# Values and keys of the first layer projected together at the start, and 128-column products without padding, in a two-layer hybrid attention kernel

## The chip, the cores and the metric

The kernel runs on one NeuronCore of a Trainium2 chip. The metric is the device time of one execution in microseconds, the median of several runs. Where a row is quoted, PE is the matrix engine (PEld its weight loads), ACT the scalar engine, DVE the vector engine, POOL the GpSimd engine and SP the engine whose queue issues the DMAs here.

## The reference, cut to what matters

Two layers, 512 positions, model width 1024. Each layer has one projection whose columns feed two token mixers: group A (8 heads, stick-breaking attention) and group B (8 heads, sparse attention whose keys are picked by an indexer).

```python
def hybrid_layer(x, w_in, w_out, ln_g, ln_b, rel_bias, topk):
    proj = jnp.einsum('bsd,dn->bsn', x, w_in)
    qA, kA, vA, gA, qB, kB, vB, gB, qI, kI, wI = jnp.split(proj, SPLIT_POINTS, axis=-1)
    ...
    oA = stick_breaking_attention(heads(qA, HEADS_A), heads(kA, HEADS_A), heads(vA, HEADS_A))
    oB = dsa_sparse_attention(..., qI, kI, wI, rel_bias, topk)
    mix = jnp.concatenate([oA * jax.nn.silu(gA), oB * jax.nn.silu(gB)], axis=-1)
    y = jnp.einsum('bsm,md->bsd', mix, w_out)
    return layer_norm(ALPHA * x + y, ln_g, ln_b)

# indexer, in dsa_sparse_attention: keys kI (64 columns), head weights wI (8 columns)
rel = jax.nn.relu(jnp.einsum('bqhd,bsd->bqhs', qib, k_idx))
score = jnp.einsum('bqhs,bqh->bqs', rel, wib)      # top 128 keys of each query are kept
```

## The kernel before, in words

**Numbers.** Every product is made of three fp32r products: high part by high part, low by high, high by low. A high part is a copy through ACT, a low part a subtraction on DVE or POOL. XH and XL hold x in both parts, turned, in 8 slices of 128 model columns (kc). The matrix engine loads 128 columns of weights per product and streams 128 to 512 columns past them.

**Units.** The projection is done in units of 256 columns, named by group, half and kind, such as ("A", 0, "v"), and "ki", which is the indexer's 64 key columns with its 8 head-weight columns. `project_t` (line 248) makes a unit turned, with x moving (512 columns a product, 24 products per 128 columns: 8 slices by three). `project_v` (line 259) makes values with the weights moving, 256 columns a product and 96 products a unit. In the second layer (l = 1) the unit ("A", 0, "v") is made at the end of the layer before, together with the keys, as 256 + 72 = 328 moving columns; its split weights lie in `joined`, a view on the AT tiles. In the first layer (l = 0) the keys are a unit of their own of 72 weight columns and the values come later among the fills.

**Start of the first layer** (`first_units`, line 351). Nine products on zeros run first. Then x, the key weights and the two halves of ("I", 0, "q") are loaded in pieces (1, 1, 2, 2, 2 slices) and split and multiplied slice by slice into three accumulators (two of `ppj`, one of `po`). `evac_ki` and `evac_q` copy the results out; a copy of the keys to the other 64 partitions is a DMA (`twin`). The 8 head weights are turned by four small transposes (L484) and `signs` makes their signs and magnitudes.

**Slots.** After `fill(0)`, a layer runs 24 index slots and 64 attention slots. Slot s issues two products z (L430, L433: queries against keys, n = 128 (qb + 1) columns but at least 256), and the older blocks' transposes and copies. Four blocks make a head, whose values product (L599) is eight products of 512, 384, 256 and 256 columns; the last pair needs only 128, and the rest of it is held at zero by four memsets in `constants`. Between them `fill` issues projection steps up to a target that `pins` sets: a unit (16 steps of three products) is to be done by the slot in HEAD_PINS, A_PINS (another row for each layer) and B_PINS; `PREFILL = 6` steps go ahead of slot 0.

**Values of group A** are differences of neighbouring rows: `shift_values` moves the copy V_NOW by one row into V_PREV with three DMAs, and `value_steps` (SHIFT_SLOTS = 2 slots later) subtracts on DVE and splits. The order on PE, ACT, DVE and POOL is the order of the code; the SP queue's is set by the scheduler. Weights are loaded two pieces ahead (`Stream`).

```python
accs = [ppj.tile([P, S], F32, tag="pj", name="pj") for _ in range(2)]
...
nn = max(self.n, 256)
...
pins = [(0, PREFILL * 648)]
```

Of the kernel before, what the change touches and what calls it, by code (L numbers as in the profile page):

```python
# [49 lines left out]
PREFILL = 6  # L50
# [7 lines left out]
A_PINS = ((27.8, 31.2, 35, 38.2, 42, 45.4, 48.4, 51.4, 54.2, 56.8), (29, 32.5, 36, 40, 44, 47.4, 50.6, 53.8, 56.8))  # L58
SHIFT_SLOTS = 2
# [4 lines left out]
def fills(l):  # L64

    units = [("I", 1, "q"), ("A", 0, "k"), ("A", 0, "q")]
    units += [("A", 0, "v")] * (l == 0)
# [3 lines left out]
    return list(zip(units, HEAD_PINS + A_PINS[min(l, 1)] + B_PINS, strict=True))  # L71


UNITS = [("I", 0, "q")] + [u for u, _ in fills(0)]
# [18 lines left out]
def tile_hybrid(ctx: ExitStack, tc: tile.TileContext, xt, x, w_in, w_ki, w_out, ln_g, ln_b, rel_bias, onehot, out, depth=DEPTH):  # L93
# [119 lines left out]
    def units(l):  # L213
        u = [u for u, _ in fills(l)]
        return ["ki", ("I", 0, "q")] + u if l == 0 else [("A", 0, "v"), "ki", ("I", 0, "q")] + u

    specs, index = [], {}
    for l in range(depth):
        for unit in units(l):
# [28 lines left out]
    def project_t(l, unit, evac):  # L248
        n = 72 if unit == "ki" else P
        for c in range(1 if unit == "ki" else 2):  # L250
            w = stream.get(index[l, unit] + c)
            acc = ppj.tile([P, S], F32, tag="pj", name="pj")[:n]
            for kc in range(KC):
                mm3(acc, [t[:, kc * n : (kc + 1) * n] for t in w], kc, kc == 0, kc == KC - 1)
# [4 lines left out]
    def project_v(l, unit, vt, keys=None):  # L259
# [9 lines left out]
        for tb in range(NTB):  # L269
# [4 lines left out]
            for kc in range(KC):  # L274
# [11 lines left out]
                if (tb, kc) == (NTB - 1, KC - 1) and unit[0] == "A":  # L286
                    later.append(shift_values)
                    pending.append([SHIFT_SLOTS, lambda: value_steps(vv)])
# [62 lines left out]
    def first_units(evac_ki, evac_qi):  # L351
        done = []
        raws = kp.tile([P, 4, S], F32, tag="k", name="raws").rearrange("p a b -> p (a b)")
        raws = [vp.tile([P, NTB, 4 * P], F32, tag="v", name="raw0").rearrange("p a b -> p (a b)"), raws[:, :1024], raws[:, 1024:]]
        for i in range(3):
            done.append(tuple(wp.tile([P, 1024], F32R, tag=tag, name=f"{tag}{i}") for tag in ("whi", "wlo")))
        bias["oh"] = kp.tile([P, 4, S], F32, tag="k", name="oh").rearrange("p a b -> p (a b)")
        accs = [ppj.tile([P, S], F32, tag="pj", name="pj") for _ in range(2)]
# [5 lines left out]
        accs.append(po.tile([P, S], F32, tag="o", name="pjo"))  # L364
        cuts = [0, 1, 2, 4, 6, 8]
        for a, b in zip(cuts, cuts[1:]):
            load_x(a, b - a)
            for i in range(3):
                n = specs[i][1] // 8
                nc.sync.dma_start(raws[i][:, a * n : b * n], specs[i][0][:, a * n : b * n])  # L370
        stream.loaded = stream.ready = 3
        stream.load(4)
        for a, b in zip(cuts, cuts[1:]):
            for kc in range(a, b):
                split_x(kc)
                if kc == a:
                    for i in range(3):
                        n = specs[i][1] // 8
                        c = slice(a * n, b * n)
                        split(done[i][0][:, c], done[i][1][:, c], raws[i][:, c], lo_engine=G)  # L380
                for i in range(3):
                    n = specs[i][1] // 8
                    mm3(accs[i][:n], [t[:, kc * n : (kc + 1) * n] for t in done[i]], kc, kc == 0, kc == KC - 1)
            if a == 0:
                constants()
            if b == 6:
                stream.prep(3, V)
        for i in range(3):
            stream.done[i] = done[i]
        evac_ki(0, accs[0][:72])  # L390
        for c in range(2):
            evac_qi(c, accs[c + 1])
        stream.prep(4)
# [28 lines left out]
    class Block:  # L422
# [3 lines left out]
        def product(self, q, slot, k, ks, mask=None, cols=None, spare=False):  # L426
            nn = max(self.n, 256)
# [567 lines left out]
```

## Time and profile before

| | |
|---|---|
| median of 3 runs | 664.27 us (663.07 to 664.74) |
| the profiled execution | 663.7 us, of which the span is 661.9 us |
| granted PE clock | 0.997 of full |
| PE busy | 650.0 us, 98% of the span, 3549 products |
| DVE, ACT, POOL busy | 73%, 53%, 55% |
| start: first product on data to first z of slot 0 | 4.65 to 29.07 us |
| z products, first layer, first to last | 29.1 to 292.4 us |
| z products, second layer, first to last | 364.6 to 615.4 us |

A product's duration in a row overlaps its neighbours (0.39 us for one of 512 columns); what it costs in a row of products is the distance from its start to the next start. "Idle before" is time in which the engine stood still.

### The profile page before, as it was taken

To read this page: it belongs to the slowest core of one execution; us is meant where nothing else is said; L and a number is where in the kernel's file an instruction comes from. 1 tells how busy PE (TensorE), PEld (TensorE's weight loads), DVE (VectorE), ACT (ScalarE), POOL (GpSimd) and SP (SyncE) were. 2 spreads that over 40 slices of the span, in tenths; PEclk is the share of its full clock that TensorE was granted. 3 is DMA by queue.
4 is the path that set the end of the run, shared out by engine and by line. 5 is a ranking of instruction groups with operands and counts; after the bars stand their busy time and mean duration, and the time that the engine had idled before them with its cause. 6 is when DMAs were issued, how large, how long until landed. Compare 5 with 4: busy or idle time off the path is not lost.

```text
span 661.9 us, 10351 instructions
## 1 busy us (share of the span) xinstructions
PE 650.0 (98%) x3549; PEld 552.7 (83%) x3549; DVE 483.2 (73%) x1026; ACT 351.3 (53%) x708; POOL 361.7 (55%) x345
## 2 busy tenths in 40 slices
PE   8999999999999999999999999999999999999995
PEld 4778988988889989878898888889888898897785
DVE  3588989999956455656853789999989565556577
ACT  4586445544346566884133865544534566668700
POOL 5343634466575767788124435445466566677621
PEclk9999999999999999999999999999999999999998
DMA  7625224142243454343004242332124424442202
GB/s 260 219 79 150 97 96 127 65 128 82 78 144 97 135 125 154 101 153 98 25 21 123 97 130 94 128 96 96 64 64 144 127 81 154 138 138 71 96 33 95
DMA packets 27115, 72.85 MB, mean 110 GB/s; under 512 B 5140, under 2 KB 8084, under 8 KB 27064
## 3 DMA queue, kind: packets, MB, share of 16 engines
q1 hardware_dynamic: 27064, 72.20, 34.5%
q8 instruction: 28, 0.46, 0.3%
q14 instruction: 23, 0.19, 0.1%
HBM read 58.87 MB, written 2.31 MB: 92 GB/s over the span
## 4 chain that ended last, share of the span: by engine, by line
PE 80%; ACT 6%; DVE 6%; POOL 3%; issue 2%; DMA 2%; SPq 1%; DVEq 0%; POOLq 0%; ACTq 0%
PE pj L244 14%; PE pj L246 14%; PE pj L245 14%; PE o L599 5%; PE tr L438 4%; PE pjv L276 4%; PE pjv L277 4%; PE pjv L278 4%; PE pjo L697 4%; PE pjo L695 4%; PE pjo L694 4%; PE z L430 4%; PE z L433 3%; POOL wlo L195 2%; ACT whi L193 1%
## 5 line engine op out<-in xcount | busy, mean ns | idle before, releaser
L195 POOL TENSOR_TENSOR wlo<-raw,whi 128x512 fp32r<-128x512 f32 x158 | 215.1, 1383 | 131.2 <-ACT whi L193 125.3
L244 PE MATMUL pj<-XH,whi 128*128 128x512 f32 (+1 forms) x448 | 182.3, 407 | 0.0
L245 PE MATMUL pj<-XL,whi 128*128 128x512 f32 (+1 forms) x448 | 175.5, 392 | 1.1 <-DVE XL L149 1.1
L246 PE MATMUL pj<-XH,wlo 128*128 128x512 f32 (+1 forms) x448 | 175.8, 392 | 0.0
L246 PEld LDWEIGHTS pj<-XH,wlo 128*128 128x128 f32 (+1 forms) x448 | 83.7, 187 | 19.6 <-POOL wlo L149 0.4
L245 PEld LDWEIGHTS pj<-XL,whi 128*128 128x128 f32 (+1 forms) x448 | 84.2, 188 | 14.9 <-DVE XL L149 2.7
L244 PEld LDWEIGHTS pj<-XH,whi 128*128 128x128 f32 (+1 forms) x448 | 84.0, 188 | 14.0 <-ACT whi L148 0.7
L193 ACT ACTIVATE whi<-raw 128x1024 fp32r<-128x1024 f32 x80 | 84.1, 1054 | 4.9 <-DMA raw<-in_w_in_dram 3.3
L618 DVE TENSOR_TENSOR_SCAN om<-om 128x128 f32<-128x128 f32 (+1 forms) x64 | 71.2, 1113 | 5.8 <-POOL om L614 5.6
L612 ACT ACTIVATE om<-z 128x128 f32<-128x128 f32 (+1 forms) x64 | 28.0, 437 | 87.2 <-PE z L433 82.9
L276 PE MATMUL pjv<-whi,XH 128*128 128x256 f32 x224 | 66.3, 296 | 0.0
L278 PE MATMUL pjv<-wlo,XH 128*128 128x256 f32 x224 | 63.2, 282 | 0.0
L277 PE MATMUL pjv<-whi,XL 128*128 128x256 f32 x224 | 63.2, 282 | 0.0
L510 POOL TENSOR_TENSOR M<-M,mixt 64x512 f32<-64x512 f32 x22 | 32.0, 1454 | 47.3 <-DVE mixt L509 41.3
L741 DVE MAX8 m<-scores 128x8 f32<-128x256 f32 (+2 forms) x96 | 52.8, 550 | 0.2
L742 DVE MATCH_REPLACE8 scores<-m,scores 128x256 f32<-128x256 f32 (+2 forms) x96 | 52.1, 543 | 0.0
L614 POOL TENSOR_SCALAR_AFFINE_SELECT om<-om 128x128 f32<-128x128 f32 x64 | 22.9, 359 | 52.4 <-ACT om L612 46.4
L599 PE MATMUL o<-AT,vt 128*128 128x256 f32 (+2 forms) x256 | 48.3, 328 | 0.7 <-DVE AT L449 0.5
L599 PEld LDWEIGHTS o<-AT,vt 128*128 128x128 f32 x256 | 41.8, 188 | 6.7 <-DVE AT L449 1.5
L694 PE MATMUL pjo<-whi,XH 128*128 128x512 f32 (+1 forms) x118 | 46.3, 393 | 0.0
L449 DVE TENSOR_TENSOR AT<-tr,AT 128x128 fp32r<-128x128 f32 (+1 forms) x64 | 31.3, 489 | 20.5 <-ACT AT L446 20.0
L697 PE MATMUL pjo<-wlo,XH 128*128 128x512 f32 (+1 forms) x118 | 44.8, 380 | 0.0
(153 smaller groups left out, 1313.1 us busy)
## 6 DMA issues: line engine op xcount, KB each, us to landing
raw<-in_w_in_dram SPq DMA_DIRECT2D x68, 512.0 KB, 3.3
k<-k SPq DMA_DIRECT2D x32, 256.0 KB, 5.3
raw<-in_w_out_dram SPq DMA_DIRECT2D x14, 512.0 KB, 3.3
gbias<-f_dram SPq DMA_DIRECT2D x16, 256.0 KB, 6.1
XN<-in_x_dram SPq DMA_DIRECT2D x4, 512.0 KB
M<-M SPq DMA_DIRECT2D x4, 448.0 KB
out_dram<-XN SPq DMA_DIRECT2D x7, 256.0 KB
XN<-in_xt_dram SPq DMA_DIRECT2D x3, 512.0 KB
```

The costliest lines, as they stand in the source:

```text
L193: A.activation(hi, src, AF.Copy)
L195: lo_engine.tensor_tensor(lo[:, c], src[:, c], hi[:, c], ALU.subtract)
L244: T.matmul(o, w[0], XH[:, :, kc, :], start=first, stop=False)
L245: T.matmul(o, w[0], XL[:, :, kc, :], start=False, stop=False)
L246: T.matmul(o, w[1], XH[:, :, kc, :], start=False, stop=last)
L276: T.matmul(full, XH[:, tb, kc, :], whi, start=kc == 0, stop=False)
L277: T.matmul(full, XL[:, tb, kc, :], whi, start=False, stop=False)
L278: T.matmul(full, XH[:, tb, kc, :], wlo, start=False, stop=kc == KC - 1)
L599: T.matmul(self.o[:, q0 * P :], vt[:, sb, self.hh * P : (self.hh + 1) * P], at_block(self.at[j], sb, q0, NTB - q0), start=n == 0, stop=n == 7)
L618: V.tensor_tensor_scan(rev, rev, rev, 1.0, ALU.mult, ALU.min)
L694: T.matmul(acc[:, cols], XH[:, tb, m, :], whi, start=n == 0, stop=False)
L697: T.matmul(acc[:, cols], XH[:, tb, m, :], wlo, start=False, stop=n == 2 * len(mts))
```

## The change

Three things change. First, the first layer begins with ("A", 0, "v") and the keys together, 328 columns with the weights moving, and ("I", 0, "q") beside them, all three loaded, split and multiplied slice by slice; the unit "ki" of 72 weight columns, the four small transposes and the fill of ("A", 0, "v") go, four transposes of the keys come in. The signs are made as soon as the keys are out. Second, the value steps of that unit run at slot 14, both layers have one row of A_PINS, and the first layer's PREFILL is 8. Third, products whose result is 128 columns wide stream 128 columns instead of 256, and the memsets of the padding go.

```diff
-PREFILL = 6
+PREFILL = (8, 6)
...
-A_PINS = ((27.8, 31.2, 35, 38.2, 42, 45.4, 48.4, 51.4, 54.2, 56.8), (29, 32.5, 36, 40, 44, 47.4, 50.6, 53.8, 56.8))
-SHIFT_SLOTS = 2
+A_PINS = (29, 32.5, 36, 40, 44, 47.4, 50.6, 53.8, 56.8)
+SHIFT_SLOTS = (14, 2)
...
-        for i in range(2):
-            for j in range(2):
-                V.memset(at_block(AT[i][j], 3, 2, 1).bitcast(F32), 0.0)
...
+        cuts = [0, 1, 2, 3, 4, 6, 8]
         for a, b in zip(cuts, cuts[1:]):
             load_x(a, b - a)
+            half, at = specs[unit[0] + a // 4][0], a % 4
+            nc.sync.dma_start(vk_raw[:, a:b, :W256], half[:, at * W256 : (at + b - a) * W256].rearrange("p (a b) -> p a b", b=W256))
+            nc.sync.dma_start(vk_raw[:, a:b, W256:], specs[unit[1]][0][:, a * 72 : b * 72].rearrange("p (a b) -> p a b", b=72))
+            nc.sync.dma_start(q_raw[:, :, a * P : b * P], q_src[:, :, a * P : b * P])
...
+        def product(j, kc, w, q):
+            x = (XH, XL, XH)[j]
+            first, last = kc == 0 and j == 0, kc == KC - 1 and j == 2
+            for tb in range(NTB) if q is None else ():
+                T.matmul(full[tb], x[:, tb, kc, :], w[j // 2][:, kc % 4, :], start=first, stop=last)
+            for c in q or ():
+                T.matmul(q_accs[c].rearrange("p (a b) -> p a b", b=P), q_w[c][j // 2][:, kc * P : (kc + 1) * P], x[:, :, kc, :], start=first, stop=last)
...
+            if b >= 6:
+                stream.prep(stream.ready, V if b == 6 else G)
+        for j in range(3):
+            product(j, KC - 1, w, None)
+        for tb in range(NTB):
+            V.tensor_copy(keys[:, tb, :], full[tb][:, W256:])
+            A.activation(V_NOW[:, tb, :], full[tb][:, :W256], AF.Copy)
+        shift_values()
+        head_weights()
+        for c in range(2):
+            for j in range(3):
+                product(j, KC - 1, w, (c,))
+            if c == 0:
+                turn_keys(keys)
+        for c in range(2):
+            evac_qi(c, q_accs[c])
...
-            nn = max(self.n, 256)
+            nn = self.n
...
-                for n, (sb, q0, j) in enumerate((sb, q0, j) for sb, q0 in ((0, 0), (1, 1), (2, 2), (3, 2)) for j in range(2)):
+                for n, (sb, q0, j) in enumerate((sb, q0, j) for sb, q0 in ((0, 0), (1, 1), (2, 2), (3, 3)) for j in range(2)):
...
         if l == 0:
-            first_units(evac_ki, lambda c, p: evac_q(qi, c, p))
+            first_units(nxt["keys"], turn_keys, head_weights, lambda c, p: evac_q(qi, c, p))
+            pending.append([SHIFT_SLOTS[0], lambda: value_steps(nxt["v"].rearrange("p t (a r) -> p t a r", r=256))])
```

**Order on PE, one slice of the start.** Before, the nine products of a slice (pj of 72 rows are the keys, the others the two halves of the queries):

```order
L244 MATMUL pj<-XH,whi_124 72x512
L245 MATMUL pj<-XL,whi_124 72x512
L246 MATMUL pj<-XH,wlo_125 72x512
L244 MATMUL pj<-XH,whi_126 128x512
L245 MATMUL pj<-XL,whi_126 128x512
L246 MATMUL pj<-XH,wlo_127 128x512
L244 MATMUL pjo<-XH,whi_128 128x512
L245 MATMUL pjo<-XL,whi_128 128x512
L246 MATMUL pjo<-XH,wlo_129 128x512
```

Now the 18 of a slice (AT_105 and AT_106 are the split weights of values and keys, whiq and wloq those of the queries):

```order
L378 MATMUL pjv<-AT_105,XH 128x328 x4
L380 MATMUL pjq<-XH,whiq_125 128x512
L380 MATMUL pjq<-XH,whiq_127 128x512
L378 MATMUL pjv<-AT_105,XL 128x328 x4
L380 MATMUL pjq<-XL,whiq_125 128x512
L380 MATMUL pjq<-XL,whiq_127 128x512
L378 MATMUL pjv<-AT_106,XH 128x328 x4
L380 MATMUL pjq<-XH,wloq_126 128x512
L380 MATMUL pjq<-XH,wloq_128 128x512
```

Three products of the keys became twelve that make the keys and the values.

**Order on PE, end of the start.** Before, behind the fills ahead of slot 0 (tw are the head weights, z the first products of slot 0):

```order
L244 MATMUL pj<-XH,whi_274 128x512
L245 MATMUL pj<-XL,whi_274 128x512
L246 MATMUL pj<-XH,wlo_275 128x512
L484 MATMUL tw<-ident,wt 128x8 x4
L430 MATMUL z<-ki,q 128x256
L433 MATMUL z<-ki,q 128x256
```

Now, the last slice (pk are the keys, turned):

```order
L378 MATMUL pjv<-AT_107,XH 128x328 x4
L378 MATMUL pjv<-AT_107,XL 128x328 x4
L378 MATMUL pjv<-AT_108,XH 128x328 x4
L380 MATMUL pjq<-XH,whiq_125 128x512
L380 MATMUL pjq<-XL,whiq_125 128x512
L380 MATMUL pjq<-XH,wloq_126 128x512
L496 MATMUL pk<-ident,keys 64x128 x4
L380 MATMUL pjq<-XH,whiq_127 128x512
L380 MATMUL pjq<-XL,whiq_127 128x512
L380 MATMUL pjq<-XH,wloq_128 128x512
L238 MATMUL pj<-XH,whi_336 128x512
```

The transposes stand between the last products of the two halves of the queries; 24 fill products follow them, and then the first z, where there were 18 fill products and the four small transposes.

**Order on SP, from the last loads of the start to the copy of the keys.** Before:

```order
L174 DMA raw_166<-in_w_in_dram 128x1024
L174 DMA raw_168<-in_w_in_dram 128x1024
L415 DMA XN<-in_x_dram 128x1024 x2
L174 DMA raw_279<-in_w_in_dram 128x1024
L415 DMA XN<-in_x_dram 128x1024 x2
L152 DMA ki<-ki 64x1024
```

Now (M<-M are the three moves of `shift_values`):

```order
L170 DMA raw_172<-in_w_in_dram 128x1024
L170 DMA raw_174<-in_w_in_dram 128x1024
L435 DMA XN<-in_x_dram 128x1024 x2
L170 DMA raw_341<-in_w_in_dram 128x1024
L435 DMA XN<-in_x_dram 128x1024
L170 DMA raw_376<-in_w_in_dram 128x1024
L435 DMA XN<-in_x_dram 128x1024
L292 DMA M<-M 1x16x48
L290 DMA M<-M 112x1024
L291 DMA M<-M 15x1024
L148 DMA ki<-ki 64x1024
```

The copy of the keys now stands behind the three moves of the values and one more load of weights.

## Rows read from the trace of the kernel before

**Rows 1.** The profile page: busy time of PE, and the chain of work that ended last, by engine.
```profile
PE 650.0 (98%) x3549; PEld 552.7 (83%) x3549; DVE 483.2 (73%) x1026; ACT 351.3 (53%) x708; POOL 361.7 (55%) x345
...
PE 80%; ACT 6%; DVE 6%; POOL 3%; issue 2%; DMA 2%; SPq 1%; DVEq 0%; POOLq 0%; ACTq 0%
```
**Rows 2.** Busy time by stretch (us from the span's start): the start; a stretch of the second layer's first attention slots. Columns: length, then PE, PEld, DVE, ACT and POOL busy, granted PE clock, DMA share, GB/s.
```profile
4.60:29.05 24.45, 23.09 (x96) 15.76 (x94) 13.14 (x26) 12.52 (x28) 13.13 (x18) 1.00 0.81 280
400.00:425.00 25.00, 25.00 (x120) 20.60 (x119) 24.45 (x56) 13.13 (x23) 13.91 (x17) 1.00 0.26 87
```
**Rows 3.** Timeline of PE in the start (start us, us, instruction): the first product on data, two of a row of four equal ones (three starts apart), and the small transposes with slot 0's first product.
```profile
4.65 0.92 PE L244 MATMUL pj<-XH,whi 128*72 128x512 f32 x1
...
8.69 0.39 PE L246 MATMUL pj<-XH,wlo 128*72 128x512 f32 x1
...
9.37 0.39 PE L246 MATMUL pj<-XH,wlo 128*128 128x512 f32 x1
...
28.73 0.41 PE L484 MATMUL tw<-ident,wt 8*128 8x8 f32 x4
29.07 0.38 PE L430 MATMUL z<-ki,q 128*128 128x256 f32 x1
```
**Rows 4.** Who waited for whom in the start, 4.6 to 29 us: engine and line, what it waited for, us in total, times, longest.
```profile
ACT whi L193 <- DMA raw<-in_w_in_dram: 3.3, 1, 3.3
PEld pj L245 <- DVE XL L149: 2.7, 4, 1.2
```
**Rows 5.** Timeline of PE in the second layer's values with keys: products of 328 columns, 38 apart, the four transposes of its keys, and the second of the 512-column products behind them.
```profile
343.20 0.32 PE L276 MATMUL pjv<-AT,XH 128*128 128x328 f32 x1
...
348.95 0.32 PE L278 MATMUL pjv<-AT,XH 128*128 128x328 f32 x1
...
350.48 0.60 PE L474 MATMUL pk<-ident,keys 128*64 128x128 f32 x4
...
351.15 0.39 PE L245 MATMUL pj<-XL,whi 128*128 128x512 f32 x1
```
**Rows 6.** Timeline of ACT in the start: when the pieces of x and the weights came and what a split costs.
```profile
3.73 0.63 ACT L148 ACTIVATE XH<-XN 128x512 fp32r<-128x512 f32 x1 [1.71 <-DMA XN<-in_xt_dram]
...
5.05 0.31 ACT L148 ACTIVATE whi<-raws 128x128 fp32r<-128x128 f32 x1 [0.34 <-DMA raws<-in_w_in_dram]
9.57 0.63 ACT L148 ACTIVATE XH<-XN 128x512 fp32r<-128x512 f32 x1 [2.15 <-DMA XN<-in_xt_dram]
...
17.04 1.06 ACT L193 ACTIVATE whi<-raw 128x1024 fp32r<-128x1024 f32 x1 [3.31 <-DMA raw<-in_w_in_dram]
```
**Rows 7.** The second layer's keys and values: copies out (ACT), the moves and the copy of the keys (SP, issue times), the value steps (DVE).
```profile
349.57 0.39 ACT L283 ACTIVATE M<-pjv 128x256 f32<-128x256 f32 x1 [2.29 <-DVE keys L281]
351.12 0.59 ACT L467 ACTIVATE ki<-pk 64x512 fp32r<-64x512 f32 x1 [0.22 <-PE pk L474]
...
346.35 0.58 SPq L299 DMA_DIRECT2D M<-M  x1
350.30 0.55 SPq L297 DMA_DIRECT2D M<-M  x1
350.90 0.89 SPq L298 DMA_DIRECT2D M<-M  x1
...
351.74 0.68 DVE L468 TENSOR_TENSOR ki<-pk,ki 64x512 fp32r<-64x512 f32 x1 [1.95 <-ACT ki L467]
357.90 1.22 DVE L302 TENSOR_TENSOR M<-M 128x1024 f32<-128x1024 f32 x1
359.82 1.29 DVE L308 TENSOR_TENSOR vt<-M,vt 128x512 fp32r<-128x512 f32 x2 [0.70 <-ACT vt L306]
```
**Rows 8.** DMA issues: count, KB each, median us from issue to landing.
```profile
k<-k SPq DMA_DIRECT2D x32, 256.0 KB, 5.3
ki<-ki SPq DMA_DIRECT2D x2, 256.0 KB, 3.0
```
**Rows 9.** Timeline of PE in two attention slots of group B, first an fp32r product of 256 columns, then a bf16 product (the mask) of 128 columns in the first slot and of 256 in the second, then (left out) the second fp32r product of 256 columns, and the transposes.
```profile
267.70 0.28 PE L430 MATMUL z<-k,q 128*128 128x256 f32 x1
267.82 0.23 PE L432 MATMUL z<-mask,identb 128*128 128x128 bf16 x1
...
268.06 0.49 PE L438 MATMUL tr<-ident,p 128*128 128x128 f32 x3
...
269.82 0.28 PE L430 MATMUL z<-k,q 128*128 128x256 f32 x1
269.94 0.28 PE L432 MATMUL z<-mask,identb 128*128 128x256 bf16 x1
...
270.18 0.60 PE L438 MATMUL tr<-ident,p 128*128 128x128 f32 x4
```
**Rows 10.** Timeline of PE where plain fp32 (not fp32r) goes over 128 columns: one product, which has two records.
```profile
40.05 0.38 PE L408 MATMUL pf<-oh 32*8 32x128 f32 x2
```
**Rows 11.** The z products of each layer (L430), duration and first and last start: the index slots and the attention slots of the first layer, then of the second.
```profile
L430 PE MATMUL z<-k,q x64: 276/308/403, 68.1 to 292.4; 128*128 128x256 f32 x32, 128*128 128x384 f32 x16, 128*128 128x512 f32 x16
L430 PE MATMUL z<-ki,q x24: 278/337/446, 29.1 to 56.1; 128*128 128x256 f32 x8, 128*128 128x384 f32 x8, 128*128 128x512 f32 x8
...
L430 PE MATMUL z<-k,q x64: 276/308/403, 401.8 to 615.4; 128*128 128x256 f32 x32, 128*128 128x384 f32 x16, 128*128 128x512 f32 x16
L430 PE MATMUL z<-ki,q x24: 277/335/397, 364.6 to 389.8; 128*128 128x256 f32 x8, 128*128 128x384 f32 x8, 128*128 128x512 f32 x8
```

More of the change, by code (lines that the diff above doesn't have):

```diff
@@ L70, in fills @@
     units += [("B", 0, "v"), ("B", 1, "k"), ("B", 1, "q"), ("B", 1, "v")]
-    return list(zip(units, HEAD_PINS + A_PINS[min(l, 1)] + B_PINS, strict=True))
-UNITS = [("I", 0, "q")] + [u for u, _ in fills(0)]
+    return list(zip(units, HEAD_PINS + A_PINS + B_PINS, strict=True))
+UNITS = [("A", 0, "v"), ("I", 0, "q")] + [u for u, _ in fills()]
 def unit_col(u):
@@ L211, in prep_ahead @@
             self.prep(self.want)
-    def units(l):
-        u = [u for u, _ in fills(l)]
-        return ["ki", ("I", 0, "q")] + u if l == 0 else [("A", 0, "v"), "ki", ("I", 0, "q")] + u
+    units = [("A", 0, "v"), "ki", ("I", 0, "q")] + [u for u, _ in fills()]
     specs, index = [], {}
     for l in range(depth):
-        for unit in units(l):
+        for unit in units:
             index[l, unit] = len(specs)
@@ L376, in first_units @@
                 if kc == a:
[L377 to L383, printed above, removed]
+                    split(w[0][:, a % 4 : a % 4 + b - a, :], w[1][:, a % 4 : a % 4 + b - a, :], vk_raw[:, a:b, :], lo_engine=G)
+                    for c in range(2):
+                        A.activation(q_w[c][0][:, a * P : b * P], q_raw[:, c, a * P : b * P], AF.Copy)
+                    for c in range(2):
+                        G.tensor_tensor(q_w[c][1][:, a * P : b * P], q_raw[:, c, a * P : b * P], q_w[c][0][:, a * P : b * P], ALU.subtract)
+                if kc < KC - 1:
+                    for j in range(3):
+                        product(j, kc, w, None)
+                        product(j, kc, w, range(2))
             if a == 0:
                 constants()
[L386 to L390, printed above, removed]
-        for c in range(2):
-            evac_qi(c, accs[c + 1])
-        stream.prep(4)
+            if b >= 6:
[7 more added lines that the diff above has]
+        head_weights()
+        for c in range(2):
+            for j in range(3):
+                product(j, KC - 1, w, (c,))
+            if c == 0:
+                turn_keys(keys)
+        for c in range(2):
+            evac_qi(c, q_accs[c])
     bias = {}
@@ L451, in tile_hybrid, with new_values @@
     turn = {"at": 0}
+    nxt = {}
+    def new_values():
+        nxt["v"] = vp.tile([P, NTB, 4 * P], F32R, tag="v", name="vt")
+        nxt["keys"] = tp.tile([P, S], F32, tag="t", name="keys")[:, : NTB * 72].rearrange("p (a b) -> p a b", b=72)
     def layer(l):
@@ L474, in turn_keys @@
                 T.transpose(p[:64, tb * P : (tb + 1) * P], keys[:, tb, :64], ident)
[L475 removed]
+            evac_ki(p)
         def head_weights():
[L478 to L487 removed]
+            tv = nxt["keys"][:, :, 64:]
             V.tensor_scalar(sgn, tv, 0.0, 2.0, ALU.is_ge, ALU.mult)
@@ L702, in layer @@
         queue, total = [], 0
-        pins = [(0, PREFILL * 648)]
-        for unit, by in fills(l):
+        pins = [(0, PREFILL[min(l, 1)] * 648)]
+        for unit, by in fills():
             total += 16 * 648
@@ L765, in layer @@
         fill(0)
[L766 removed]
+        if l:
+            head_weights()
         o0 = index[l, "o"]
@@ L928, in layer @@
             unit = ("A", 0, "v")
[L929 to L930 removed]
+            new_values()
             gen = project_v(l + 1, unit, nxt["v"], nxt["keys"])
```

65 lines of the change are left out of this document (24 added, 41 removed).

## The prediction

> **What bounds the kernel now.** I read the page first: PE is busy for 98% of the span and holds 80% of the chain that ended last [rows 1]. So the question is what PE has to do and where it stands still. By stretches, the start (4.6 to 29 us) is where it stands still: 23.1 us busy of 24.45, with the DMA engines 81% busy at 280 GB/s, and the clock is full there [rows 2]. The timeline gives what a product costs in a row: 512 columns, three starts in 0.68 us, 0.227 us [rows 3]; 328 columns, 38 starts in 5.75 us, 0.151 us [rows 5]; 256 columns, 0.120 us from one start to the next [rows 9]. These lie on a line of 0.107 us per 256 columns.
>
> From the first product on data (4.65) to slot 0's first z (29.07) are 24.42 us [rows 3]. In it are 8 slices of 9 products and 18 fill products, 90 by 0.227 = 20.43, and the small transposes, 0.34 [rows 3]. The rest, 3.65 us, is PE waiting: for low parts of x on DVE, which come late because ACT waits for x and for the next weights [rows 4, 6]. From slot 0 on, PE waits for almost nothing: the first layer takes 263.3 us from its first to its last z, the second 250.8 [rows 11], and the 12.5 between them are the 96 values products that the first makes there (96 by 0.120 = 11.5) and the bias table. That both layers pace alike in spite of different pins says that pins and DVE (24.45 of 25 us busy in the first attention slots [rows 2]) do not set the pace; PE's work does.
>
> **The change, part by part.** Sum against the profiled execution, 663.7 us.
>
> *Keys without products of their own.* 24 products of 512 columns go: 24 by 0.227 = 5.45 us less.
>
> *Values earlier and wider.* 96 products of 256 columns become 96 of 328: 96 by (0.151 - 0.120) = 3.0 us more. The second layer's rows price them exactly, since it makes the same product [rows 5].
>
> *Transposes.* The small ones go (0.34 [rows 3]); four of the keys come, priced by the second layer's: 351.15 - 350.48 less one product of 0.227 = 0.44 [rows 5]. Together 0.1 more.
>
> *The waits of the start.* A slice is now 12 by 0.151 and 6 by 0.227 = 3.17 us of PE where it was 2.04, while its data grow from 420 to 548 KB, 1.96 us at 280 GB/s [rows 2]. PE becomes the slowest. I check the places where it could still wait. The third slice of x is the ninth DMA as before, when the ninth had come by 9.57 [rows 6]; PE wants it at 5.1 + 2 by 3.17 = 11.4, and ACT needs 0.63 for x, some 0.46 for 328 columns (estimate between 0.31 for 128 and 0.63 for 512) and 0.62 for the queries in between [rows 6]. The next weights came at 17.04 [rows 6]; 1.05 MB more ahead of them is 3.7 us, so 20.8; their split (1.06), then x's and the pair of slices behind it bring the seventh slice to about 23.3, and PE wants it at 24.1. So the 3.65 us go; what could stay is 1.5 at most, if those weights are that much later. The memsets that go were DVE's; that is counted here.
>
> *A later first product.* ACT has x's first high part at 4.36 and the last weights piece came at 5.05 [rows 6]. Values and keys are now the second and third DMA, so they are in before that: some 4.6 plus 0.46 = 5.1, 0.45 later than now. Bounds: 0, and 0.9 if the pieces come as late as the fourth does.
>
> *The copy of the keys and the SP queue.* This is what is late next. The last values product ends at 5.1 + 7 by 3.17 + 1.8 = 29.1. ACT copies the values out (4 by 0.39), so 30.7; then SP issues the three moves, 0.58, 0.55 and 0.89 [rows 7], and only at 32.7 the copy of the keys, whose parts are ready at 32.0 (0.59 on ACT and 0.68 on DVE behind the copies [rows 7]). It lands 3.0 us later, as that copy does now, or 5.3, as the copies of other keys do in pairs [rows 8]: 35.7 to 38.0. PE reaches slot 0 at 29.1 + 6 by 0.227 + 0.44 + 24 by 0.227 = 36.35. The wait is 0 to 1.65; I take 0.7, nearer to the row of that very copy. PREFILL = 8 is already in it: with 6 steps PE would be there 1.4 us earlier. Behind z on PE is everything, so this wait counts in full.
>
> *Value steps at slot 14, signs at once.* 1.22 and 1.29 us of DVE [rows 7] move between index scores. Four relu tiles give PE a lead of about three slots, which are 27.0/23 = 1.17 us each [rows 11], 3.5 us against 2.5. Cost nothing; without that cover up to 2.5. The signs leave DVE's way before slot 0; PE did not wait for them. The splits of these weights leave POOL's and ACT's fills; both have room.
>
> *128 columns for 256.* Per layer and head, two z products and the last two values products: 128 products. No fp32r product under 256 columns is in the trace. The nearest row is the mask product: of 128 columns it and the second z take 268.06 - 267.82 = 0.24 us, of 256 columns 270.18 - 269.94 = 0.24 [rows 9]. Half the columns saved nothing there, because the fp32r product behind must load its weights, and that does not hide behind 128 columns. In the changed order 110 of the 128 stand ahead of an fp32r product, 12 ahead of transposes and 6 ahead of the mask. I give the 110 nothing and the 18 up to half a 256-column step, 0.053: 0 to 0.95, taken as 0.5 less. Bounds from farther rows: 128 by 0.053 = 6.8 less if nothing but columns counted, and 128 by 0.107 = 13.7 more if a narrow product cost what one of 512 does.
>
> The Trainium skill ("TensorE: Matmul & The Clock Gate", section "Back-to-back issue gap") gives about 81 ns per product for a stream of loads and products at 128 columns; by it this term would be, as an estimate, 128 by 0.039 = 5.0 us less and the time 654.2. The same page, section "LDWEIGHTS (loading the stationary operand)", has a load take its columns divided by 1.2 GHz, 107 ns for 128, which would leave an estimated 128 by 0.013 = 1.7 less and 657.5; the mask rows [rows 9] are on the side of this second rule.
>
> Sum: -5.45 + 3.0 + 0.1 - 3.65 + 0.45 + 0.7 - 0.5 = -5.35, so 658.35. A second way: slot 0 at 37.05, then 250.8 as in the second layer, plus 1.0 for the bias table, less two steps made ahead (1.36), puts the last z of the first layer at 287.5 instead of 292.4: 4.9 less, and 0.5 for the narrow products, 5.4. The profiled execution lies 0.6 under the median of the runs shown, within their spread; I add half of that: **658.7 us**.
>
> **The rivals.**
>
> *Narrow fp32r products are slow (slower than before).* One mechanism, in every first block and every values product: below 256 columns fp32r loses its rate. For it: on this engine a plain fp32 product of 128 columns has two records that last 0.38 us, where an fp32r one of 256 columns lasts 0.28 [rows 9, 10], so a rate per type exists; and nothing in the trace shows fp32r narrow. Against: the mask and three transposes of 128 columns (0.49 us together) show no such step [rows 9]. Price 0.107 each as for 512 columns: 658.7 + 0.5 + 13.7 = 672.9. It decides from (5.35 - 0.5)/128 = 0.038 on: the change is slower if a 128-column product takes more than 0.158 us.
>
> *The waits come back.* The copy of the keys lands at 38.0 (0.95 more than counted) and the value steps at slot 14 hold z for their 2.5 us: 658.7 + 3.45 = 662.1. For: DVE was at its limit later on, SP issues in order. Against: the lead of three slots.
>
> *Narrow products are cheap.* Only columns count: 0.120 - 0.053 = 0.067 us each, so 6.8 less in place of 0.5, 652.4. For: from 512 to 256 columns the price falls by columns alone. Against: the mask rows, directly. The Trainium skill's section "Back-to-back issue gap" leads most of the way here, to its 654.2.
>
> **How the numbers follow.** The forecast 0.71, slow narrow products 0.11, returning waits 0.13, cheap narrow products 0.05. About 0.3% (2 us) is what a measurement of this kernel can tell from no change. Returning waits reach less than 2 us of gain in about half of their cases: faster 0.71 + 0.05 + 0.07 = 0.83, same 0.06, slower 0.11. The forecast's best end (no later first product, no wait for the keys, 0.95 for the narrow products) is 6.95 less, about 657.0; its worst (0.9, 1.65, nothing for the narrow ones, 1.5 of waits left) is 1.95 less, 662.0. With the runs' own spread I give 656.2 to 662.2, which takes in the returning waits and leaves out the two cases on narrow products, 0.16.
>
> **What would show it.** The first z of slot 0 at 36 to 38 us, the last z of the first layer near 287.5; first products on data near 5.1 and no PE wait of over 0.3 us from there to 29; PE waiting for the copy of the keys under 1 us; a narrow z or values product starting 0.11 to 0.12 us before the next fp32r one. Starts 0.2 us apart would make the prediction wrong on the slow side, 0.07 on the other; a first z after 39 or PE waiting for relu near slot 14 would say that the waits came back.

## The result and the profile after

The changed kernel takes 661.18 us (median of 5 runs, 660.61 to 661.96), the kernel before, beside it on the same chip, 664.74 (663.07 to 665.5): ratio 0.9949, 95% interval 0.9938 to 0.996. That is 3.6 us faster, where 5.6 were forecast (664.27 to 658.7); 661.18 lies inside the range, 2.5 above the forecast. The two profiled executions differ by less than the medians do (spans 660.2 and 661.9 us): the one of after is the slowest of its five, the one of before lies under the median of its runs. A second run of the same kernel (below) gave 661.54.

PE's share on the page, against [rows 1]:

```profile
PE 646.4 (98%) x3521; PEld 551.8 (84%) x3525; DVE 481.7 (73%) x1025; ACT 350.9 (53%) x709; POOL 358.2 (54%) x344
...
PE 73%; DVE 11%; ACT 7%; issue 4%; POOL 3%; DMA 1%; DVEq 0%; POOLq 0%; ACTq 0%
```

PE's busy time went down by 3.6 us (four of the 3525 products have no record here), and its share of the chain from 80% to 73%: more of the chain now runs through DVE. The busy time by stretch, for the start (here to 37.10 us, when PE has finished the fills ahead of slot 0) and the same attention stretch as in [rows 2]:

```profile
4.60:37.10 32.50, 32.50 (x174) 28.88 (x172) 13.58 (x29) 16.28 (x36) 18.74 (x22) 1.00 0.82 272
400.00:425.00 25.00, 25.00 (x123) 20.64 (x122) 24.44 (x54) 13.43 (x24) 12.50 (x16) 1.00 0.32 105
```

PE is busy for all 32.5 us: the 3.65 us of waits of the start are gone, with the DMA engines 82% busy (81% before). The timeline of PE, with the counterparts of [rows 3] and [rows 5], and the places where it now waits:

```profile
4.77 1.53 PE L378 MATMUL pjv<-AT,XH 128*128 128x328 f32 x4
...
6.79 0.77 PE L378 MATMUL pjv<-AT,XL 128*128 128x328 f32 x4
...
29.23 0.76 PE L378 MATMUL pjv<-AT,XH 128*128 128x328 f32 x4
...
36.91 0.39 PE L240 MATMUL pj<-XH,wlo 128*128 128x512 f32 x1
38.76 0.36 PE L450 MATMUL z<-ki,q 128*128 128x256 f32 x1 [1.46 <-DMA ki<-ki]
...
60.36 0.44 PE L450 MATMUL z<-ki,q 128*128 128x384 f32 x1 [0.25 <-ACT relu L557]
...
84.98 0.33 PE L458 MATMUL tr<-ident,om 128*128 128x128 f32 x1 [0.52 <-DVE om L631]
```

Four products of 328 columns take 1.53 us at first and 0.77 from 6.79 us on, so PE began at the lower of its two rates. The granted clock of that stretch reads 1.00 all the same: at the start of a run the column does not show the slow rate, only the products' times do. PE was ready for the first z at 36.91 + 0.23 = 37.14 and got it at 38.76, 1.62 us later, behind the copy of the keys. Who waited for whom in that stretch, against [rows 4]:

```profile
ACT whi L189 <- DMA raw<-in_w_in_dram: 3.1, 1, 3.1
...
PE z L450 <- DMA ki<-ki: 1.5, 1, 1.5
```

The line "PEld pj <- DVE XL" of before is gone; ACT still waits 3.1 us for the next weights, but PE no longer waits behind it. SP's issues at the end of the start show why the keys are late:

```profile
30.97 0.62 SPq L292 DMA_DIRECT2D M<-M  x1
31.64 0.58 SPq L290 DMA_DIRECT2D M<-M  x1
32.26 0.93 SPq L291 DMA_DIRECT2D M<-M  x1
33.30 1.06 SPq L148 DMA_DIRECT2D ki<-ki  x1
```

The copy is issued at 33.30 (forecast 32.7), and z starts 5.46 us after that (forecast 3.0 to 5.3). The z products of each layer, against [rows 11]:

```profile
L450 PE MATMUL z<-k,q x64: 220/308/450, 77.3 to 291.0; 128*128 128x128 f32 x16, 128*128 128x256 f32 x16, 128*128 128x384 f32 x16, 128*128 128x512 f32 x16
L450 PE MATMUL z<-ki,q x24: 278/371/497, 38.8 to 65.3; 128*128 128x256 f32 x8, 128*128 128x384 f32 x8, 128*128 128x512 f32 x8
...
L450 PE MATMUL z<-k,q x64: 220/308/442, 400.4 to 613.8; 128*128 128x128 f32 x16, 128*128 128x256 f32 x16, 128*128 128x384 f32 x16, 128*128 128x512 f32 x16
L450 PE MATMUL z<-ki,q x24: 277/335/398, 363.1 to 388.4; 128*128 128x256 f32 x8, 128*128 128x384 f32 x8, 128*128 128x512 f32 x8
```

The first layer takes 252.2 us from its first to its last z of this line (263.3 before), the second 250.7 (250.8 before). The first z comes 9.7 us later and the last one of the first layer 1.4 us earlier. Against before's 263.3 less 96 by 0.120 for the values and 1.36 for two steps made ahead, 250.4, the first layer is 1.8 us long, and three waits in it hold 1.4: 0.36 us at 43.5 us, 0.52 at 60.36 and 0.74 at 84.98, less the 0.22 that the second layer has at the last place. These waits and those for relu and DVE below are taken from the ends of neighbouring products, against the same products in a row without a wait; the idle time in brackets is 0.2 to 0.3 us less.

### The profile page after: what moved, and what is told of

Same layout as the page of the kernel before. It is cut to its first block, busy times and chain, and to the rows that moved or that the text cites. A ratio compares the mean times of both kernels' runs of the same rounds, so it can differ in the third digit from the quotient of the medians.

```text
span 660.2 us, 10292 instructions
## 1 busy us (share of the span) xinstructions
PE 646.4 (98%) x3521; PEld 551.8 (84%) x3525; DVE 481.7 (73%) x1025; ACT 350.9 (53%) x709; POOL 358.2 (54%) x344
## 4 chain that ended last, share of the span: by engine, by line
PE 73%; DVE 11%; ACT 7%; issue 4%; POOL 3%; DMA 1%; DVEq 0%; POOLq 0%; ACTq 0%
PE pj L238 11%; PE pj L240 11%; PE pj L239 11%; PE o L612 4%; PE tr L458 4%; PE pjo L707 4%; PE pjo L710 4%; PE pjo L708 4%; PE pjv L269 3%; PE pjv L271 3%; PE pjv L270 3%; PE z L453 3%; PE z L450 3%; PE pjv L378 2%; DVE scores L755 2%
## 5 line engine op out<-in xcount | busy, mean ns | idle before, releaser
L238 PE MATMUL pj<-XH,whi 128*128 128x512 f32 x432 | 177.2, 410 | 0.0
L240 PE MATMUL pj<-XH,wlo 128*128 128x512 f32 x432 | 169.6, 393 | 0.0
L239 PE MATMUL pj<-XL,whi 128*128 128x512 f32 x432 | 168.9, 391 | 0.0
L240 PEld LDWEIGHTS pj<-XH,wlo 128*128 128x128 f32 x432 | 81.1, 188 | 18.5
L238 PEld LDWEIGHTS pj<-XH,whi 128*128 128x128 f32 x432 | 81.4, 188 | 12.3
L239 PEld LDWEIGHTS pj<-XL,whi 128*128 128x128 f32 x432 | 81.7, 189 | 11.4
L269 PE MATMUL pjv<-whi,XH 128*128 128x256 f32 x192 | 57.8, 301 | 0.0
L271 PE MATMUL pjv<-wlo,XH 128*128 128x256 f32 x192 | 54.2, 282 | 0.0
L270 PE MATMUL pjv<-whi,XL 128*128 128x256 f32 x192 | 54.1, 282 | 0.0
L612 PE MATMUL o<-AT,vt 128*128 128x512 f32 (+3 forms) x256 | 46.0, 319 | 1.1 <-DVE vt L315 0.7
```

The source lines that it names most:

```text
L238: T.matmul(o, w[0], XH[:, :, kc, :], start=first, stop=False)
L239: T.matmul(o, w[0], XL[:, :, kc, :], start=False, stop=False)
L240: T.matmul(o, w[1], XH[:, :, kc, :], start=False, stop=last)
L269: T.matmul(full, XH[:, tb, kc, :], whi, start=kc == 0, stop=False)
L270: T.matmul(full, XL[:, tb, kc, :], whi, start=False, stop=False)
L271: T.matmul(full, XH[:, tb, kc, :], wlo, start=False, stop=kc == KC - 1)
```

## The experiments

All are timed beside the kernel before, whose median was 664.66 us beside after_again, keys_first, prefill_11 and pad_back, 664.67 beside prefill_5, before_narrow, keys_apart and keys_first_22, 664.40 beside keys_first_18 and steps_on_pool, and 664.39 beside steps_apart. Ratios are to that kernel.

**The change once more** (after_again), for a second profile.

> The changed kernel once more, as the base for the others of this batch. Theory (the gain is cut by the wait for the copy of the keys): its time again about 0.5% under the kernel before, and again a wait of 1 to 1.7 us ahead of the first z of slot 0, because the copy of the keys always stands behind the three moves on SP. Rival (the wait and the late rise of the clock belonged to that one profile): the wait is under 0.5 us here. The clock's rise came at 5.3 us in the profile of before and at 6.5 in that of the change; a third value would show that it moves from run to run by itself, 0.7 us of the start.

661.54 us (661.24 to 661.79), ratio 0.9954 [0.9941, 0.9966]. Here the first z came at 38.27, 1.1 us after PE was ready. The wait is there again, and its size moves by half a microsecond. The slow beginning is there again too: 1.46 us for the first four products.

**The copy of the keys ahead of the large moves** (keys_first). The values are moved two slots later:

```diff
-        shift_values()
         head_weights()
...
+            pending.append([2, shift_values])
             pending.append([SHIFT_SLOTS[0], lambda: value_steps(nxt["v"].rearrange("p t (a r) -> p t a r", r=256))])
```

> The three moves of the values are put off to slot 2, so that the copy of the keys is the first of them on SP. Theory: the copy is issued at some 32.6 instead of 33.3 us and has the DMA engines to itself, lands by 36, and the wait ahead of the first z (1.5 us) goes: 1.3 to 1.7 us less than the changed kernel. Rival (the copy is slow for another reason, such as the weights and x loads that run at the time): it lands as late, no change. Rival (wait only moves): the first z is earlier, but the index slots wait 1 us more for relu and the total stays.

660.20 us (660.0 to 660.66), ratio 0.9934 [0.9922, 0.9947], 1.3 us under the change run beside it. SP's issues and PE's first z in this kernel, a fence each:

```profile
32.16 0.51 SPq L148 DMA_DIRECT2D ki<-ki  x1
32.72 0.58 SPq L419 DMA_DIRECT2D oh<-in_rel_bias_dram  x1
33.34 0.62 SPq L290 DMA_DIRECT2D M<-M  x1
34.01 0.94 SPq L291 DMA_DIRECT2D M<-M  x1
```

```profile
5.30 0.86 PE L378 MATMUL pjv<-AT,XH 128*128 128x328 f32 x4 [0.56 <-ACT AT L144]
...
36.55 0.39 PE L240 MATMUL pj<-XH,wlo 128*128 128x512 f32 x1
36.77 0.28 PE L449 MATMUL z<-ki,q 128*128 128x256 f32 x1
```

Issued 1.1 us earlier and ahead of the 448 KB of the moves, the copy is there before PE asks, at most 4.6 us after its issue (5.0 to 5.5 behind the moves); the z follows the last fill by 0.22 us, one product. The first z comes 1.5 us earlier than in the second profile of the change (38.27), and the span is 1.5 us shorter (658.2 and 659.7). So the wait was the queue's doing and counted in full. Here PE ran the first four products at the full rate (0.86 us with small gaps), and the start up to the first z took 31.47 us from 5.30, against 32.37 from 4.77 to 37.14 in the change's profile, which began at the lower rate.

**Three more fill steps ahead of slot 0** (prefill_11), `PREFILL = (11, 6)`, cover for the same wait.

> Eleven projection steps instead of eight ahead of slot 0, three of 0.68 us, work that is only made earlier. Theory: 2.04 us of work cover the wait of 1.5 us, so 1.3 to 1.7 us less than the changed kernel, the copy landing at the same time as in it. Rival (the eleven need the weights of the second piece, whose low part POOL ends late): a new wait on POOL of 0.5 us or more. Rival (index slots get too thin): with 5 fill steps in the first eleven slots PE waits for relu or scores there, and the gain is under 0.5 us.

661.49 us (661.22 to 661.81), ratio 0.9954 [0.9941, 0.9966]: the change's time. PE's timeline:

```profile
38.87 0.28 PE L450 MATMUL z<-ki,q 128*128 128x256 f32 x1
...
43.54 0.50 PE L450 MATMUL z<-ki,q 128*128 128x512 f32 x1 [1.48 <-ACT relu L557]
```

The first z no longer waits, but 4.7 us later another one waits 1.75 us, for relu, which ACT does behind two splits of weights: the second rival. The steps that cover one wait are missing as cover at the next.

**Three steps fewer** (prefill_5), `PREFILL = (5, 6)`.

> The change with 5 fill steps ahead of slot 0 in place of 8, so 9 products of 512 columns fewer ahead of the first z, made later among the slots. My theory, that the first z waits for the copy of the keys, which lands when it lands: the first z stays at 38.3 to 38.8 us, its wait grows by 2.04 us from 1.2 to 1.7 to 3.2 to 3.7, and the three steps come back later: 1.4 to 2.0 us slower than the change, 662.9 to 663.5 us. Rival, that PE's own work sets the first z and the wait seen there is small change: the first z comes 2.04 us earlier, near 36.5 us, and the time is that of the change, 661.5.

664.16 us (661.81 to 666.12, 12 runs), ratio 0.9993 [0.9979, 1.0007]: 2.6 us slower than the change, more than expected and with a wide spread. PE's timeline and then its granted clock by stretch (seventh group of numbers, behind the five engines):

```profile
35.13 0.39 PE L240 MATMUL pj<-XH,wlo 128*128 128x512 f32 x1
37.83 0.45 PE L450 MATMUL z<-ki,q 128*128 128x256 f32 x1 [2.31 <-DMA ki<-ki]
...
38.29 0.63 PE L238 MATMUL pj<-XH,whi 128*128 128x512 f32 x1
38.72 0.63 PE L239 MATMUL pj<-XL,whi 128*128 128x512 f32 x1
...
42.13 0.39 PE L239 MATMUL pj<-XL,whi 128*128 128x512 f32 x1
```

```profile
37.80:40.00 2.20, 2.17 (x7) 1.91 (x8) 0.35 (x1) 1.42 (x2) 0.00 (x0) 0.53 0.00 0
40.00:42.00 2.00, 2.00 (x8) 1.68 (x7) 0.45 (x1) 0.58 (x1) 1.98 (x2) 0.66 0.00 0
42.00:44.00 2.00, 2.00 (x12) 1.73 (x11) 0.49 (x1) 1.65 (x4) 0.67 (x1) 1.00 0.19 31
```

The first z stays where the copy lands (37.83), so the copy sets it, as expected. What was not expected: after 2.5 us of standing still PE goes on at the lower rate, 0.43 us from one 512-column product to the next where 0.23 is usual, for about 3.5 us. By the granted clock that loses 2.2 by (1 - 0.53) and 2.0 by (1 - 0.66), 1.7 us. In the change itself the wait was 1.6 us and the granted clock stayed at 1.00, as it did after the 1.75 us in prefill_11. Of the twelve runs three lie at 661.8 to 662.3, with a mean granted clock of 0.997 or 0.998, and nine at 663.9 to 666.1, with 0.991 to 0.996. Only the first of the twelve has a profile; by these means the clock held in three runs, and there the three steps cost only 0.3 to 0.7 us, less than the 1.4 to 2.0 expected. Why they cost so little was not shown.

**The padding back** (pad_back): the change with 256 columns and the memsets.

```diff
-            nn = self.n
+            nn = max(self.n, 256)
...
-((0, 0), (1, 1), (2, 2), (3, 3))
+((0, 0), (1, 1), (2, 2), (3, 2))
```

> The changed kernel with 256 columns again where the result is 128 wide, and the memsets of the padding back. Theory (a product of 128 columns gives its time back to the weight load of the next): 0 to 0.6 us slower than the changed kernel, same within the measurement; from the two traces, two z products and the next of 512 columns end 470 ns after what stood ahead of them with 128 columns and 477 with 256, so 64 pairs by 7 ns, 0.45 us. Rival (narrow products are slow and ate a part of the gain): 1.5 us or more faster than the changed kernel. Rival (they count by columns): 6 us slower.

661.85 us (661.46 to 662.23), ratio 0.9958 [0.9945, 0.9972], 0.3 above the change beside it, which is within the noise. The first pair of group A between two 512-column products, in the change and then with the padding:

```profile
77.33 0.22 PE L450 MATMUL z<-k,q 128*128 128x128 f32 x1
77.38 0.28 PE L453 MATMUL z<-k,q 128*128 128x128 f32 x1
77.50 0.45 PE L238 MATMUL pj<-XH,whi 128*128 128x512 f32 x1
77.78 0.39 PE L239 MATMUL pj<-XL,whi 128*128 128x512 f32 x1
```

```profile
76.42 0.28 PE L453 MATMUL z<-k,q 128*128 128x256 f32 x1
76.54 0.28 PE L456 MATMUL z<-k,q 128*128 128x256 f32 x1
76.66 0.40 PE L241 MATMUL pj<-XH,whi 128*128 128x512 f32 x1
76.89 0.40 PE L242 MATMUL pj<-XL,whi 128*128 128x512 f32 x1
```

Two narrow products start only 0.05 us apart, which looks like columns saved. But the wide product behind them takes 0.28 us to the next start instead of 0.23, and from the first z to the second wide product it is 0.45 against 0.47 us. The saving is repaid within three products. The weight loads of that stretch start at 77.33, 77.44 and 77.55 us, 0.11 apart, and that is what a narrow product costs. So starts of neighbours don't price a product; the distance over the whole group does.

**The narrow columns alone** (before_narrow), on the kernel before.

> The kernel before with the third part of the change alone: results of 128 columns stream 128 columns, and the four memsets of the padding are gone; the start, the pins and the value steps are those of before. My theory, that a product of 128 columns costs no less than 0.112 to 0.114 us because the weights of the next one load behind it: 0 to 0.6 us faster than before, 664.1 to 664.7 us. Rivals: only columns count, 6.8 us faster, 657.9; narrow fp32r products lose their rate, 13.7 us slower, 678.4.

663.54 us (662.59 to 664.22, 11 runs), ratio 0.9984 [0.9976, 0.9993]: 1.1 us faster, 0.5 to 1.6 by the interval, a little more than expected. The two other prices (6.8 less, 13.7 more) are out.

**The keys as products of their own** (keys_apart), on keys_first: values of 256 columns, and per slice three products of 72 weight columns for the keys, with the old small transposes.

```diff
-        full = [t[:, : W256 + 72] for t in accs]
+        full = [t[:, :W256] for t in accs]
...
+                T.matmul(k_acc.rearrange("p (a b) -> p a b", b=P), w[j // 2][:, kc % 4, W256:], x[:, :, kc, :], start=first, stop=last)
```

> On the version with the copy of the keys ahead of the large moves (keys_first, 660.20 us), the indexer's keys are again made apart: 24 products of 72 weight columns with x moving (512 columns), and the values alone with 256 moving columns, with the four small transposes of the head weights in place of the four of the keys; everything is still loaded and split as in the change. My theory, that PE's work counts in full in a start where it no longer waits: 24 by 0.227 = 5.45 us more, 96 by (0.151 - 0.120) = 3.0 less, transposes 0.1 less, so 2.35 us slower: 662.5 us. First rival, that the start is bounded by the arrival of the data or by the splits on ACT: no change, 660.2. Second rival, that values and keys together save only the loads of weights that hide anyway and 328 columns cost more than 0.151 in this place: the difference is under 1 us.

663.03 us (662.69 to 663.58, 10 runs), ratio 0.9976 [0.9967, 0.9986]: 2.8 us above keys_first. PE's timeline in one slice of this kernel, and at its first z:

```profile
18.85 0.64 PE L379 MATMUL pjv<-AT,XH 128*128 128x256 f32 x4
19.33 0.39 PE L381 MATMUL pjk<-XH,AT 128*72 128x512 f32 x1
19.56 0.62 PE L383 MATMUL pjq<-XH,wloq 128*128 128x512 f32 x2
20.02 0.64 PE L379 MATMUL pjv<-AT,XH 128*128 128x256 f32 x4
...
40.07 0.28 PE L452 MATMUL z<-ki,q 128*128 128x256 f32 x1
```

A third of a slice takes 20.02 - 18.85 = 1.17 us; by the forecast's prices the change's takes 4 by 0.151 + 2 by 0.227 = 1.06. 24 of these differences are 2.6 us. In a start without waits, PE's products count one for one.

**The value steps at slot 22, at slot 18, and on POOL** (keys_first_22, keys_first_18, steps_on_pool), each on keys_first: `SHIFT_SLOTS = (22, 2)`, `(18, 2)`, and the subtraction and low parts by POOL at slot 14.

> On the version with the copy of the keys ahead of the large moves (keys_first, 660.20 us), the value steps run at slot 22 in place of slot 14. My theory, that these steps put the index slots' relu late once and PE waits 0.52 us for it at 58.3 us: that wait goes and, where the scores of the last index slots are not as tight, none takes its place: 0.3 to 0.5 us faster, 659.7 to 659.9. Rival, that DVE has no room at slot 22 either, where the first of its scans are near: the wait moves there, 660.2 or up to 1 us more. Second rival, that the wait at 58.3 us is not due to the steps: no change and the wait stays.

> On keys_first (660.20 us), the value steps at slot 18, on DVE. At slot 14 they cost PE 0.52 us at once and left 0.74 us at 83.0 us; at slot 22 nothing at once and 1.67 us at 83.3 us. My theory, that DVE's 2.5 us have no cover from slot 14 to the end of the index scores and only change the place at which PE pays: the two waits together stay at 1.2 to 1.7 us, 660.2 to 660.6 us. Rival, that there is slack between the two places: both waits are under 0.8 us together, 659.7 or less.

> On keys_first (660.20 us), the subtraction and the low parts of the first layer's first values step, at the same slot 14, are done by POOL in place of DVE; the two copies stay on ACT. My theory: DVE's 2.5 us of these steps are paid twice on PE, as 0.52 us at 58.3 us, where relu is late, and as some 0.5 us at 83.0 us, where DVE has worked without a gap since 68 us and PE waits 0.74 us for a scan (0.22 in the second layer). POOL stands idle from 53.3 to 60.3 us and needs about 2.5 + 2.6 us for the same elements (2.54 us for two of 128x512). Both waits go: 0.5 to 1.0 us faster, 659.2 to 659.7 us. Rival, that the splits of the weights on POOL come late in exchange and PE waits for a low part of weights in the fills near 62 to 66 us: 660.2 or up to 1 us more. Second rival, that the wait at 83.0 us has nothing to do with the steps: only the first goes, 659.7, and 0.74 us stay.

660.60 us (660.26 to 662.49), ratio 0.9945 [0.9931, 0.996], at slot 22; 660.41 (660.11 to 661.18), 0.9943 [0.9931, 0.9956], at slot 18; 661.24 (661.06 to 661.45), 0.9954 [0.994, 0.9967], on POOL. The first two cannot be told from keys_first by these intervals; on POOL, where I expected a gain, it is a loss of 1.0 us. At slot 22 the wait near 58 us goes, but the one at 83 us grows from 0.74 to 1.67, as the first rival had it. At slot 18 there is 0.84 at 63.4 and still 0.74 at 83.2, together within the forecast 1.2 to 1.7. On POOL the first wait grows from 0.52 to 1.12 and the second from 0.74 to 1.48. I took that for the end of the theory that DVE's 2.5 us of work are paid on PE, since DVE had been relieved of them. But it had not been relieved. One step of the scores on DVE, 384 columns, in keys_first; then with the steps on POOL, beside POOL's subtraction:

```profile
54.98 0.61 DVE L566 SCALAR_TENSOR_TENSOR scores<-relu,sgn,scores 128x384 f32<-128x384 f32 x1
```

```profile
54.78 2.57 POOL L295 TENSOR_TENSOR M<-M 128x1024 f32<-128x1024 f32 x1
...
55.03 2.74 DVE L566 SCALAR_TENSOR_TENSOR scores<-relu,sgn,scores 128x384 f32<-128x384 f32 x1
```

Beside the moved steps three score steps of DVE took 2.74, 0.91 and 1.65 us, which take 0.61, 0.48 and 0.61 where POOL stands idle: 3.6 us lost for 2.5 saved. So this run does not decide on that theory; ACT's queue and the experiment behind it do. (Nor was POOL free from 53.3 us: it split weights until 54.77.) ACT's timeline in keys_first, and then with the steps on POOL:

```profile
56.75 1.16 ACT L299 ACTIVATE vt<-M 128x512 fp32r<-128x512 f32 x2 [3.38 <-DVE M L295]
```

```profile
57.39 1.15 ACT L299 ACTIVATE vt<-M 128x512 fp32r<-128x512 f32 x2 [3.98 <-POOL M L295]
58.45 1.51 ACT L556 ACTIVATE relu<-z,absw 128x256 f32<-128x256 f32 x3
```

ACT stands for 3.4 to 4.0 us in front of its two copies, waiting for the subtraction, with the relu tiles queued behind them.

**The copies two slots after the subtraction** (steps_apart), on keys_first:

```diff
-            pending.append([SHIFT_SLOTS[0], lambda: value_steps(nxt["v"].rearrange("p t (a r) -> p t a r", r=256))])
+            pending.append([SHIFT_SLOTS[0], subtract_rows])
+            pending.append([SHIFT_SLOTS[0] + 2, lambda: low_steps(nxt["v"].rearrange("p t (a r) -> p t a r", r=256))])
```

> On keys_first (660.20 us): the subtraction of the first layer's first values step stays at slot 14 on DVE, but the two copies on ACT and the low parts on DVE run two slots later. With the steps on POOL the wait at the same place had grown from 0.52 to 1.12 us though DVE was relieved, so my theory of DVE's 2.5 us fell. New theory: ACT stands still for 3.38 us behind the subtraction (its copies wait for it, and its relu tiles are queued behind them), so relu is late; with the copies two slots (2.3 us) later that idle time shrinks below 1.5 us, and the wait of PE near 58.3 us goes: 0.3 to 0.5 us faster, 659.7 to 659.9 us; the 0.74 us at 83.0 us stay, as DVE does the same work. Rival, that it is the sum of ACT's and DVE's work, not the order, that makes relu late: the wait moves by two slots and stays at 0.5 us or more, 660.2 to 660.6 us.

659.03 us (658.92 to 659.46), ratio 0.992 [0.9906, 0.9933], 1.2 under keys_first (0.9 if each is taken by its distance to the kernel before beside it) and the fastest version here. ACT's and PE's timelines of this kernel:

```profile
57.10 1.15 ACT L305 ACTIVATE vt<-M 128x512 fp32r<-128x512 f32 x2 [1.02 <-DVE M L299]
...
82.46 0.33 PE L463 MATMUL tr<-ident,om 128*128 128x128 f32 x1 [0.18 <-DVE om L636]
```

ACT now waits 1.02 us for the subtraction (and 1.3 us for scores, with relu tiles done in between), the wait of PE near 58 us is gone, and the one at 83 us fell from 0.74 to 0.40, which I had not expected. The first layer is 0.8 us shorter, 251.4 for 252.2. DVE does the same work as in keys_first, so near 58 us it is not DVE's 2.5 us that PE paid for: it is the order on ACT that made relu late.

## Why the prediction was right, and what it missed

The range held, and with it the main steps at the start; but 661.18 lies nearer to the 662.1 of the rival "the waits come back" than to the forecast's 658.7. The first z came at 38.76 (36 to 38 forecast, and 39 was the rival's sign) after 1.6 us of waiting for the keys (under 1 forecast), and the rival's other sign came: a wait for relu, at the twentieth of the 24 index slots, behind the value steps. So the number is right because the range took in this rival, not because the middle was well aimed. The second way of the sum had the last z of the first layer at 287.5; it came at 291.0, in the slowest of the five runs. Of these 3.5 us, 0.8 were there when PE was ready for slot 0 (37.14 for 36.35), 0.9 are the copy of the keys, and 1.8 came in the slots.

What held: *Keys without products of their own, wider values and transposes*: forecast 2.35 us, measured 2.8 by undoing them (keys_apart). *The waits of the start*: forecast to go, and gone. *The first product on data*: forecast 5.1, measured 4.67 to 5.58 in the profiles with this start. *The narrow columns*: forecast 0.5 less, measured 0.3 and 1.1, the first within the noise; both rivals on their price are excluded. But my own sign for them was badly chosen: I wrote that starts 0.07 us apart would make the prediction wrong, and starts 0.05 apart came with next to nothing saved. The mask rows [rows 9] had been read over two products together, and that is why they led right. The Trainium skill ("TensorE: Matmul & The Clock Gate", section "Back-to-back issue gap") would have put a 128-column product at 81 ns; a narrow pair with the wide product behind it, 0.45 us less 0.23, gives 0.11 each here, on the side of the same page's section "LDWEIGHTS (loading the stationary operand)", 107 ns.

The term that was mis-sized is *the copy of the keys*: 0.7 taken, 1.1 to 1.6 measured, at the upper bound of 1.65. Two things made it so. In the change's profile SP issued the copy at 33.3, not 32.7, since ACT had the values out at 31.1, not 30.7, and the three moves took SP 2.3 us, not 2.0. And z came 5.0 to 5.5 us after the issue; I took the 3.0 us of that very copy [rows 8], but the row of the other keys, 5.3, was the nearer one: the copy runs here beside 448 KB of moves and two loads of 512 KB that SP had issued since 30.1. With the two large moves behind it, in keys_first, it took at most 4.6. keys_first shows the price of this order: 1.3 us.

*The value steps at slot 14* I costed at nothing, with DVE's time against four relu tiles. The wrong part was the engine: DVE's 2.5 us were covered, but ACT stood 3.4 us in its queue for DVE's result, and relu is ACT's. They cost 0.52 us at once, and splitting them off made the first layer 0.8 us shorter. There is also the 0.36 us at 43.5 us: relu behind two splits of weights in a row on ACT, whose fills I had said "have room". Together these waits come to two thirds of the rival's price, 0.9 for the keys above what was counted and 1.4 in the first layer, 2.3 of its 3.45. The median missed the forecast by 2.5.

*What I did not see at all*: PE's slow first microseconds. Of the 3.65 us that I took for waiting, 0.5 was the first product at the lower rate, 4.65 to 5.40 us; the granted clock of 1.00 [rows 2] had hidden it. With PE waiting for data they cost next to nothing: in before_narrow, whose start is that of the kernel before, PE ran slowly until 7.1 us (in before until 5.4) and its first z came at 28.94, no later than the 29.07 of before. Without these waits they count. The change's profile lost 0.9 us to it against keys_first's (32.37 and 31.47 us for the same work). prefill_11 and prefill_5, with the same instructions up to there, took 0.86 and 1.63 us for their first four products. That the moment of the full rate differs from run to run is what the same page of the Trainium skill says in its section "What you observe", and these two traces agree. That this is the cause of the spread between runs was not shown.

*The wait at 83 us* belongs to DVE. Between 68 us and that wait DVE works without a gap, and the transposes that end it start 14.5 to 14.6 us after its search for the top keys begins: 82.99 after 68.37 in keys_first, 83.29 after 68.76 at slot 22, 84.31 after 69.79 with POOL, 82.46 after 67.93 in steps_apart. So what delays this beginning is paid there: with POOL the slowed score steps; in steps_apart a wait of 0.70 us of DVE for ACT's copies is gone. What delays it at slot 22 was not isolated.

## What to carry to other kernels

When an edit moves a step, follow each of its instructions into the queue of its own engine and ask what is behind it: the two losses here were a DMA behind three others on one queue, and copies waiting in order in front of work that was due. More cover (fill steps) or another slot only moved the wait, and another engine slowed the one that was to be relieved; reordering the queue removed it. Price a small product over the whole group of products around it, never by the distance of two starts.

## What the runs showed of the hardware

A wait of 2.5 us on PE was followed by 3.5 us at the lower of the two rates (granted clock 0.53 and 0.66 in the two stretches that hold it), which cost 1.7 us on top of the wait; after waits of 1.6 and 1.75 us it stayed full. So that wait cost more than one and a half times its length. The same 1024-column subtraction took 1.21 us on DVE with POOL idle, and 2.57 on POOL with DVE at work. Beside a working POOL, DVE's score step of 384 columns took 2.74 us instead of 0.61 (steps_on_pool), and one of 512 columns 1.52 instead of 0.74 (keys_first, beside a split of weights).

An fp32r product of 128 columns cost 0.11 us, against 0.12 for one of 256: half the columns save next to nothing and lose nothing.
